# Spreading projection matmuls over the steps of a decoder layer, and loading rows a few steps sooner

## The chip, the cores and the metric

The kernel runs on one core of a Trainium2 chip. The core has five engines that run on their own and meet through semaphores: TensorE (PE in the profile; its weight loads are PEld), VectorE (DVE), ScalarE (ACT), GpSimd (POOL) and SyncE (SP), which here only issues DMAs. The metric is the device time of one execution in microseconds, lower is better.

## The reference: one decoder layer

The layer takes x of 1024 positions by 1024 columns and computes

```
h = rmsnorm(x, mix_pre_norm)
q_a, k_a, v_a, q_h, f_h, i_h, g_h = split(h @ w_in)
attn = rmsnorm(dilated_mixture_attention(q_a, k_a, v_a))       # 8 heads of 64
rec  = hgrn2_recurrence(q_h, f_h, i_h, lower_bound, out_gain) * silu(g_h)   # 4 heads of 128
x = x + rmsnorm(concat[attn, rec] @ w_out)
x = x + rmsnorm(relu(rmsnorm(x) @ w_ff1)^2 @ w_ff2)
```

The attention of a head is a causal softmax over all earlier positions, with a bias per head that holds the three dilated windows and the slope of the head. The recurrence of a head keeps a 128 by 128 state, S_t = diag(f_t) S_(t-1) + (1-f_t) i_t^T, and puts out S_t^T q_t, normalised per head. All is float32.

## The kernel before

**Products.** A product of two float32 matrices is made of three matmuls (`three_pass`, lines 87 to 89): each operand is split into a high part, rounded by a copy on ACT, and a low part, the rest, subtracted on DVE (`split_into`, lines 83 and 84). The weights go through the same: `w_get(i)` makes sure that block i of the stream of weights, and one more, are split, and each split starts the load of the next block (`w_split`, `w_load`). The split weights `wh`, `wl` have two tiles each; some blocks of `w_out` go to tiles that WO_TAG names.

**Order.** The program writes every engine's order out by hand, in the order in which the Python code emits it; no scheduler changes it. Work that has no fixed place, the projections, stands in a `queue` of generators. `fill(ns)` takes pieces off that queue until they add up to ns; each piece is a few matmuls (three of 128x512 are charged 650, three of 128x256 330) and whatever must follow them. What is charged too much or too little is carried over in `debt`. `drain()` takes all that is left at once. A generator that yields None stops the filling until the next call.

**Recurrent heads.** `hgrn_core(h)` works on head h while `fill` spreads the projections of the next head (`hgrn_ig`, `hgrn_qf`) or, in the last head, of the first pair of attention heads (`attn_proj(0)`) between its parts: a fill of 4500, the diagonal products `pd` of the tile `prod` (line 379, 8 products with one column), seven levels of products `pl` (line 393) each with a fill of 2900, the transposes `pk`, the state updates `pu`, the outputs `po` in two banks, and after the norm another fill of 3000. In the last head the first scores of the attention are taken before that fill (`open_attention`).

**Attention.** The 8 heads are worked in 4 pairs, and 64 steps, one for each head and each block b of 128 queries. Step s does, in this order: the exponential of step s+1 on ACT (`raise_`, `expo`), the scores of step s+2 (`look`, `score`: `ps` on PE, then on DVE the bias added and the maximum taken, then its negative `nm`), the transposes of its own exponentials (`turn`: `pt` on PE into two banks of the tag "t", `pth` copied on ACT, `ptl` subtracted on DVE), after every second block the product with the values (`weigh`, `pov`, and its copy `ot`), and the folding and scaling of the one before (`finish`, `anat`). Then come the hooks of that step, and a fill of 2700 - 320 b, or of 1300 in the last pair. A pair ends with block 7 of its second head, so that the steps of a pair are 0 to 15, 16 to 31 and so on, and long blocks stand at the end of each head.

**Projections of a pair.** `attn_proj(pr)` makes queries, values and keys of pair pr, each in two halves of 512 positions and 24 matmuls. After each half DVE scales it (`qf`, `vf`, `kf`), ACT splits off the high parts (`q`, `kh`) and POOL the low ones (`ql`, `kl`), and SP issues small DMAs that lay them out in the other half of the partitions. The next pair's generator is put into the queue two steps before it is needed, when the pair before begins to run out: at s = 14, 30 (and for the first ones by `open_attention`), after a `drain()` that finishes the pair that is about to be scored.

**The recurrent rows.** The outputs of the recurrent heads go to memory (`mix_dram`) and are read back for the output projection. At step 45 `early_open` opens the tiles for the first four blocks of rows in the pool "wide", whose eight tiles hold `hT`, the transposed input, until the last projection is done; it loads the rows, and the bias table of head 7. `row_rec` multiplies them by their gain on POOL, `row_turn` transposes them on PE (`pmt`, also in the banks of tag "t") and splits them into `emt`, and `early_out` multiplies them with the first four blocks of `w_out` (`pwe`). These products are the filling of the last pair's steps.

The rest (the output projection, and the two products of the feed-forward part, from 585 us on) is written by other functions that the change does not touch.

Of the kernel before, what the change touches and what calls it, by code (L numbers as in the profile page):

```python
# [8 lines left out]
F32 = mybir.dt.float32  # L9
# [8 lines left out]
P = 128  # L18
# [7 lines left out]
AH = 8  # L26
# [9 lines left out]
def hymba_layer(ctx, tc, x, w_in, w_out, w_ff1, w_ff2, g_pre, lb_logits, g_mix, g_post,  # L36
# [21 lines left out]
    def half(name, dtype=F32):  # L58
        return sp.tile([P, 512], dtype, tag="half", name=name, bufs=2)
# [91 lines left out]
    for i in range(4 * HH, 4 * HH + 3 * (AH // 2)):  # L151
        stream.append((w_in[i], None))
    WO0 = len(stream)
    WO_TAG = (None, None, ("S", "S"), ("S", "BT"), ("S", "S"), ("S", "T"), ("T", "T"), ("T", "T"))

    def wo_dest(k, tags):
        return lambda: (slab(tags[0], f"woh{k}", F32R), slab(tags[1], f"wol{k}", F32R))
# [215 lines left out]
    def hgrn_core(h, scale, after=None):  # L373
        hd = heads[h]
        inat, gate, prod, qt, kt, tot = (hd[n] for n in ("inat", "gate", "prod", "qt", "kt", "tot"))
        fill(4500 * scale)
        pd = bank("t", f"pd{h}")
        for c in range(NT):
            TE.matmul(pd[:, c:c + 1], prod[:, c * P:(c + 1) * P], ones, start=True, stop=True)
# [3 lines left out]
        V.tensor_tensor(out=at, in0=ident.unsqueeze(1).to_broadcast([P, NT, P]),  # L383
                        in1=dg.unsqueeze(2).to_broadcast([P, NT, P]), op=ALU.mult)
        cur = tot
        for li, c in enumerate(LEVELS):
            nb = 64 // c
            qv = qt.rearrange("p (b two c) -> p b two c", two=2, c=c)
# [47 lines left out]
        for g4 in range(2):  # L436
            po = bank("pv", f"po{h}_{g4}").rearrange("p (n c) -> p n c", n=4)
            for j in range(4):
                n = g4 * 4 + j
                TE.matmul(po[:, j], at[:, n], inat[:, n], start=True, stop=n == 0)  # L440
                if n > 0:
                    TE.matmul(po[:, j], qt[:, n * P:(n + 1) * P], st[:, n], start=False, stop=True)
            g = slice(g4 * 4, g4 * 4 + 4)
            S.activation(sq[:, g], po, AF.Square)
            V.tensor_reduce(ss[:, g], sq[:, g], axis=AX.X, op=ALU.add)  # L445
            pos.append(po)
        rsqrt_mean(rs, ss, P, NT)
        if after is not None:
            after()
        fill(3000 * scale)  # L450
        for n in range(NT):
            V.scalar_tensor_tensor(gate[:, n], pos[n // 4][:, n % 4], rs[:, n:n + 1], gate[:, n],
                                   op0=ALU.mult, op1=ALU.mult)
# [8 lines left out]
    def attn_proj(pr):  # L462
# [48 lines left out]
        for hf in range(2):  # L511
            sl = slice(hf * 512, hf * 512 + 512)
            n = 0
            for cost in proj_t(w, f"ak{pr}", hf, box):
                n += 1
                if n == 3 and hf == 0:
                    v_turn(*late)
                    cost += 450.0
                yield cost
            full = half(f"kf{pr}{hf}")  # L520
            V.tensor_tensor(out=full, in0=box[0], in1=rrow[:, sl], op=ALU.mult)
            for i, (a, b) in enumerate(halves):
                S.activation(stacks[i]["kh"][a:b, sl], full[a:b], AF.Copy)  # L523
                G.tensor_tensor(out=stacks[i]["kl"][a:b, sl], in0=full[a:b], in1=f32(stacks[i]["kh"][a:b, sl]),  # L524
                                op=ALU.subtract)
            for n in ("kh", "kl"):
                nc.sync.dma_start(out=f32(stacks[0][n][64:128, sl]), in_=f32(stacks[0][n][0:64, sl]))
                nc.sync.dma_start(out=f32(stacks[1][n][0:64, sl]), in_=f32(stacks[1][n][64:128, sl]))
            yield 650.0
        pairs[pr] = (stacks, vs)  # L530

    anats = [None] * (AH // 2)
    bts = {}
# [2 lines left out]

    def load_bias(hd):
        if hd < AH and hd not in bts:
            if hd < AH - 1:
                bts[hd] = slab("BT", f"bt{hd}")  # L540
            else:
                bts[hd] = wide.tile([P, 2, T], F32, tag="A", name=f"bt{hd}")[:, 0]
            nc.sync.dma_start(out=bts[hd], in_=bias_tab[hd])

    def score(hd, b):
# [89 lines left out]
    NE = 4  # L635
    early = {}

    def early_open():
        early["rows"] = wide.tile([P, NE, AW], F32, tag="A", name="erows")
        early["mt"] = [wide.tile([P, 2, 2, 4, P], F32R, tag="A", name=f"emt{q}") for q in range(NE // 2)]  # L640
        load_bias(AH - 1)
        early["sum"] = [wide.tile([P, 2, D], F32, tag="A", name=f"esum{q}") for q in range(NE // 2)]
        nc.sync.dma_start(out=early["rows"],
                          in_=mix_dram[:NE * P, :AW].rearrange("(n p) d -> p n d", p=P))

    def early_sum(t):
        return early["sum"][t // 2][:, t % 2]
# [7 lines left out]
        return early["rows"][:, t] if t < NE else rows[t][:, :AW]  # L655

    def row_rec(t):
        G.tensor_tensor(out=rec_row(t), in0=rec_row(t), in1=gains["gmix"][:, :AW], op=ALU.mult)

    def row_fin(t):  # L660
        return anats[-1][:, t].rearrange("p i d -> p (i d)")
# [155 lines left out]
    for h in range(HH):  # L817
# [6 lines left out]
            drain()  # L824

    hooks = {
        45: lambda: [drain(), load_gain("gmix", "R", g_mix), early_open()],
        46: lambda: w_get(WO0, 0),
        47: lambda: [w_get(WO0 + 1, 0), row_rec(0), row_rec(1)],
        48: lambda: [row_turn(0, 0), w_get(WO0 + 2, 0), row_rec(2), row_rec(3)],  # L830
        49: lambda: [row_turn(1, 0), w_get(WO0 + 3, 0), queue.extend(early_out(t) for t in range(NE))],
        50: lambda: row_turn(2, 0),
        51: lambda: row_turn(3, 0),
        55: lambda: [row_load(t) for t in range(3)],
        59: lambda: [row_norm(0), row_gain(0)],
        60: lambda: [row_norm(1), row_gain(1)],
# [6 lines left out]
    for s in range(n_steps):  # L843
# [10 lines left out]
            to_weigh.append((hd, b // 2))  # L854
        to_fold, last_fold = [(i, g, weigh(i, g)) for i, g in ready], to_fold
        if fresh and s + 2 < n_steps:
            drain()
            if (s + 2) // 16 + 1 < AH // 2:
                queue.append(attn_proj((s + 2) // 16 + 1))
            look(s + 2)  # L860
        for i, g, a in last_fold:
            finish(i, g, *a)
        hooks.get(s, lambda: None)()
        fill(2700.0 - 320.0 * b if s < n_steps - 16 else 1300.0)
    for i, g, a in to_fold:
        finish(i, g, *a)
    to_fold = [(i, g, weigh(i, g)) for i, g in to_weigh]
# [793 lines left out]
```

## Time and profile before

| what | value |
|---|---|
| median of the runs shown | 1316.15 us (1313.2, 1319.82, 1316.15) |
| profiled execution | 1313.2 us, of which the profile's span is 1311.4 |
| PE busy over the span | 1264.5 us (96%) |
| DVE, ACT, POOL busy | 858.7, 515.1, 283.6 us |
| recurrent heads after the first projection | about 65 to 321 us |
| 64 steps of attention | about 321 to 585 us |
| HBM read, written | 106.50 MB, 39.85 MB |

Times in the profile are microseconds from the start of the span. A line of the timeline gives start, duration, engine, line of the program, operation, tile written and tiles read, shapes, and in brackets how long the engine sat idle before it and what released it; a number after an x says how many alike are merged. A line of windows gives a stretch, its length, the busy time of each engine in it with the instructions in brackets, then the granted share of the TensorE clock, the share of the DMA engines and the rate in GB/s. A line of waits says who waited for whom: microseconds in all, how often, the longest.

### The profile page before, as it was taken

Reading aid. Unit: us, or ns where it says so; the run is one execution under the profiler, and the core shown is the slowest. Engines: PE = TensorE matmul, PEld = TensorE weight load, DVE = VectorE, ACT = ScalarE, POOL = GpSimd, SP = SyncE. Lnnn points to the kernel's source line nnn. Section 1 sums busy time; section 2 is a strip of 40 time slices with the busy share of each in tenths; the row PEclk is TensorE's granted clock in tenths of the full one; section 3 lists DMA queues with packets and bytes.
Section 4 is the critical chain, followed back from the end, with each engine's and each line's share of the span. In section 5 each row is a group of like instructions: output and inputs, shape, how many; then the busy total and the mean of one; then the engine's idle time right before and its main releaser. Section 6 shows DMA issues by size and latency. Waiting matters only on the chain. (4 is left out here: it accounts for less than half of the span.)

```text
span 1311.4 us, 17500 instructions
## 1 busy us (share of the span) xinstructions
PE 1264.5 (96%) x6730; PEld 1081.8 (82%) x6730; DVE 858.7 (65%) x1431; ACT 515.1 (39%) x908; POOL 283.6 (22%) x276
## 2 busy tenths in 40 slices
PE   9999999999989999898999899999999999999997
PEld 8898989888878888786887688888887888888886
DVE  5556566675656655666757656666666777688956
ACT  6612121213545554564555422222234633344412
POOL 0000000012011111123432178755651000000002
PEclk9999999999999999899999899999999999999999
DMA  5202020213122222416251444534469453444423
GB/s 203 65 17 65 17 64 17 65 49 98 48 81 65 81 65 59 137 41 215 97 177 58 143 168 169 177 129 140 174 222 347 165 196 115 146 131 128 147 80 130
DMA packets 58563, 153.77 MB, mean 117 GB/s; under 512 B 5104, under 2 KB 13040, under 8 KB 58224
## 3 DMA queue, kind: packets, MB, share of 16 engines
q1 hardware_dynamic: 58480, 152.66, 34.9%
q8 instruction: 53, 0.87, 0.3%
q14 instruction: 30, 0.25, 0.1%
HBM read 106.50 MB, written 39.85 MB: 112 GB/s over the span
## 5 line engine op out<-in xcount | busy, mean ns | idle before, releaser
L88 PE MATMUL f<-bl,ah 128*128 128x512 f32 x392 | 152.6, 389 | 0.5 <-DVE bl L84 0.5
L87 PE MATMUL f<-bh,ah 128*128 128x512 f32 x392 | 152.6, 389 | 0.4 <-ACT acc L1441 0.4
L89 PE MATMUL f<-bh,al 128*128 128x512 f32 x392 | 152.5, 389 | 0.0
L84 DVE TENSOR_TENSOR al<-ar,ah 128x1024 fp32r<-128x1024 f32 x49 | 60.7, 1239 | 49.6 <-ACT ah L83 21.7
L88 PEld LDWEIGHTS f<-bl,ah 128*128 128x128 f32 x392 | 73.6, 188 | 16.1 <-DVE bl L84 0.8
L87 PEld LDWEIGHTS f<-bh,ah 128*128 128x128 f32 x392 | 73.6, 188 | 16.0 <-ACT acc L1441 0.9
L89 PEld LDWEIGHTS f<-bh,al 128*128 128x128 f32 x392 | 73.6, 188 | 15.3
L83 ACT ACTIVATE ah<-ar 128x1024 fp32r<-128x1024 f32 x49 | 52.3, 1067 | 54.1 <-PE f L89 25.3
L566 DVE CUSTOM_DVE_ANT_0 p<-ps,bt 128x512 f32<-128x512 f32 (+2 forms) x96 | 50.6, 552 | 31.7 <-PE ps L564 31.5
L1577 POOL TENSOR_SCALAR fp<-fss 128x1 f32<-128x1 f32 x8 | 3.5, 432 | 268.8 <-ACT fd L1574 268.8
L594 DVE TENSOR_TENSOR ptl<-pt,pth 128x512 fp32r<-128x512 f32 (+2 forms) x96 | 50.2, 551 | 16.4 <-ACT pth L593 16.3
L593 ACT ACTIVATE pth<-pt 128x512 fp32r<-128x512 f32 (+2 forms) x96 | 43.3, 486 | 42.0 <-PE pt L590 41.8
L590 PE MATMUL pt<-ident,p 128*128 128x128 f32 x288 | 43.6, 279 | 11.6 <-DVE ptl L594 11.6
L393 PEld LDWEIGHTS pl<-qt,kt 128*128 128x128 f32 x448 | 52.9, 192 | 1.5 <-PE pm_av L89 0.9
L393 PE MATMUL pl<-qt,kt 128*128 128x64 f32 x448 | 53.5, 272 | 0.5 <-DVE qt L399 0.5
L577 ACT ACTIVATE p<-p,nm 128x128 f32<-128x128 f32 (+3 forms) x64 | 49.5, 773 | 10.0 <-DVE nm L572 5.7
L524 POOL TENSOR_TENSOR kl<-kf,kh 64x512 fp32r<-64x512 f32 x16 | 20.4, 1274 | 151.3 <-ACT kh L523 150.7
L231 ACT ACTIVATE inat<-pig,rstd 128x128 f32<-128x128 f32 x32 | 11.6, 367 | 95.4 <-PE pig L89 82.3
L590 PEld LDWEIGHTS pt<-ident,p 128*128 128x128 f32 x288 | 33.7, 142 | 17.2 <-DVE ptl L594 14.2
L83 ACT ACTIVATE bh<-br 128x1024 fp32r<-128x1024 f32 x28 | 29.9, 1067 | 41.1 <-PE f L89 35.8
L79 POOL TENSOR_SCALAR ms<-hss 128x8 f32<-128x8 f32 x4 | 0.8, 196 | 203.6 <-DVE hss L445 203.6
L84 DVE TENSOR_TENSOR wl<-raw,wh 128x1024 fp32r<-128x1024 f32 x23 | 31.3, 1359 | 18.0 <-ACT wh L83 18.0
(1584 smaller groups left out, 3848.9 us busy)
## 6 DMA issues: line engine op xcount, KB each, us to landing
ar<-actd SPq DMA_DIRECT2D x49, 512.0 KB, 3.7
raw<-in_w_in_dram SPq DMA_DIRECT2D x28, 512.0 KB, 3.7
w1r<-in_w_ff_dram SPq DMA_DIRECT2D x14, 1024.0 KB, 6.5
br<-in_w_ff_dram SPq DMA_DIRECT2D x14, 1024.0 KB, 6.5
actd<-e SPq DMA_DIRECT2D x17, 768.0 KB, 4.2
actd<-e SPq DMA_DIRECT2D x11, 1024.0 KB, 4.1
xr<-in_x_dram SPq DMA_DIRECT2D x8, 512.0 KB, 9.0
bt<-in_bias_tab_dram SPq DMA_DIRECT2D x8, 512.0 KB, 4.3
```

The source lines that it names most:

```text
L83: S.activation(hi, src, AF.Copy)
L84: eng.tensor_tensor(out=lo, in0=src, in1=f32(hi), op=ALU.subtract)
L87: TE.matmul(dst, lhs[0], rhs[0], start=start, stop=False)
L88: TE.matmul(dst, lhs[0], rhs[1], start=False, stop=False)
L89: TE.matmul(dst, lhs[1], rhs[0], start=False, stop=stop)
L393: TE.matmul(pl[:, n * 64:(n + 1) * 64], kt[:, n * P:(n + 1) * P], qv[:, n * nb:(n + 1) * nb, 1, :], start=True, stop=True)
L524: G.tensor_tensor(out=stacks[i]["kl"][a:b, sl], in0=full[a:b], in1=f32(stacks[i]["kh"][a:b, sl]), op=ALU.subtract)
L566: V.tensor_tensor_reduce(out=pe[:, k0:k0 + n], in0=pS[:, :n], in1=bts[hd][:, o:o + n], scale=1.0, scalar=-3.0e38, op0=ALU.add, op1=ALU.max ...
L577: S.activation(pe[:, :nk], pe[:, :nk], AF.Exp, bias=nm[:, b:b + 1], accum_out=dn[:, b:b + 1])
L590: TE.transpose(pt[:, j * P:(j + 1) * P], pe[:, jj * P:(jj + 1) * P], ident)
L593: S.activation(hi, src, AF.Copy)
L594: V.tensor_tensor(out=lo, in0=src, in1=f32(hi), op=ALU.subtract)
```

## The change

It has three parts. In `hgrn_core` two fills are cut in two: 2200 before the products `pd` and 2300 after them, in place of 4500 before; 1500 between the two banks of `po` and 1500 after the norm, in place of 3000 after. In the steps, the fill is 3400 - 360 b in place of 2700 - 320 b, up to step 43, and 1000 in the steps 44 to 47; a pair counts as there once the first half of its keys is projected, and the steps wait with a loop of small fills for that, in place of draining. And the tiles and loads for the recurrent rows come when the first half of the last pair's keys is projected, as that frees half of `hT`'s tiles; their gain is loaded with them into half of the tile that later takes the bias table; the scaling, the transposes and the early products come one to two steps sooner, and the weight blocks of `w_out` change tiles.

```diff
-    WO_TAG = (None, None, ("S", "S"), ("S", "BT"), ("S", "S"), ("S", "T"), ("T", "T"), ("T", "T"))
+    WO_TAG = (None, ("S", "S"), None, ("S", "BT"), ("S", "S"), ("S", "T"), ("T", "T"), ("T", "T"))
...
     def hgrn_core(h, scale, after=None):
...
-        fill(4500 * scale)
+        fill(2200 * scale)
         pd = bank("t", f"pd{h}")
...
         cur = tot
+        fill(2300 * scale)
         for li, c in enumerate(LEVELS):
...
             pos.append(po)
+            if g4 == 0:
+                fill(1500 * scale)
         rsqrt_mean(rs, ss, P, NT)
         if after is not None:
             after()
-        fill(3000 * scale)
+        fill(1500 * scale)
...
     def attn_proj(pr):
...
+            if hf == 0 and pr == AH // 2 - 1:
+                early_rows()
             full = half(f"kf{pr}{hf}")
...
+            pairs[pr] = (stacks, vs)
             yield 650.0
-        pairs[pr] = (stacks, vs)
...
     def load_bias(hd):
         if hd < AH and hd not in bts:
-            if hd < AH - 1:
-                bts[hd] = slab("BT", f"bt{hd}")
-            else:
-                bts[hd] = wide.tile([P, 2, T], F32, tag="A", name=f"bt{hd}")[:, 0]
+            bts[hd] = slab("BT", f"bt{hd}") if hd < AH - 1 else early["table"][:, 0]
...
-    def early_open():
+    def early_rows():
         early["rows"] = wide.tile([P, NE, AW], F32, tag="A", name="erows")
+        early["table"] = wide.tile([P, 2, T], F32, tag="A", name="etable")
         early["mt"] = [wide.tile([P, 2, 2, 4, P], F32R, tag="A", name=f"emt{q}") for q in range(NE // 2)]
-        load_bias(AH - 1)
+        gains["early"] = early["table"][:, 1, :AW]
+        nc.sync.dma_start(out=gains["early"], in_=g_mix[:AW].partition_broadcast(P))
+        for q in range(NE // 2):
+            nc.sync.dma_start(out=early["rows"][:, 2 * q:2 * q + 2],
+                              in_=mix_dram[2 * q * P:2 * (q + 1) * P, :AW].rearrange("(n p) d -> p n d", p=P))
+
+    def early_sums():
         early["sum"] = [wide.tile([P, 2, D], F32, tag="A", name=f"esum{q}") for q in range(NE // 2)]
-        nc.sync.dma_start(out=early["rows"],
-                          in_=mix_dram[:NE * P, :AW].rearrange("(n p) d -> p n d", p=P))
...
     def row_rec(t):
-        G.tensor_tensor(out=rec_row(t), in0=rec_row(t), in1=gains["gmix"][:, :AW], op=ALU.mult)
+        gain = gains["early"] if t < NE else gains["gmix"][:, :AW]
+        G.tensor_tensor(out=rec_row(t), in0=rec_row(t), in1=gain, op=ALU.mult)
...
     hooks = {
-        45: lambda: [drain(), load_gain("gmix", "R", g_mix), early_open()],
-        46: lambda: w_get(WO0, 0),
-        47: lambda: [w_get(WO0 + 1, 0), row_rec(0), row_rec(1)],
-        48: lambda: [row_turn(0, 0), w_get(WO0 + 2, 0), row_rec(2), row_rec(3)],
-        49: lambda: [row_turn(1, 0), w_get(WO0 + 3, 0), queue.extend(early_out(t) for t in range(NE))],
-        50: lambda: row_turn(2, 0),
-        51: lambda: row_turn(3, 0),
+        45: lambda: [row_rec(0), row_rec(1)],
+        46: lambda: [w_get(WO0, 0), row_rec(2), row_rec(3)],
+        47: lambda: [row_turn(0, 0), w_get(WO0 + 1, 0), load_bias(AH - 1)],
+        48: lambda: [drain(), load_gain("gmix", "R", g_mix), early_sums(), w_get(WO0 + 2, 0), row_turn(1, 0),
+                     queue.extend(early_out(t) for t in range(NE))],
+        49: lambda: [w_get(WO0 + 3, 0), row_turn(2, 0)],
+        50: lambda: row_turn(3, 0),
...
         if fresh and s + 2 < n_steps:
-            drain()
+            while pairs[(s + 2) // 16] is None:
+                fill(1.0)
             if (s + 2) // 16 + 1 < AH // 2:
+                drain()
                 queue.append(attn_proj((s + 2) // 16 + 1))
             look(s + 2)
...
-        fill(2700.0 - 320.0 * b if s < n_steps - 16 else 1300.0)
+        fill(3400.0 - 360.0 * b if s < n_steps - 20 else 1000.0 if s < n_steps - 16 else 1300.0)
```

## The prediction, made before the changed kernel ran

> **What bounds the kernel now.** I read the page's first two parts, then busy times by stage, then the waits of TensorE (PE) in the attention stage, then the timeline at the longest of them.
>
> ```profile
> PE 1264.5 (96%) x6730; PEld 1081.8 (82%) x6730; DVE 858.7 (65%) x1431; ACT 515.1 (39%) x908; POOL 283.6 (22%) x276
> PEclk9999999999999999899999899999999999999999
> ```
>
> PE is the bound, and the total of its work is not touched: the change only reorders. So the only thing to win or lose is PE's idle time and the stretches in which its clock is granted at half (the two 8s are such slices).
>
> ```profile
> core 0: us, PE busy (x) PEld busy (x) DVE busy (x) ACT busy (x) POOL busy (x), PEclk, DMA share, GB/s
> 195.00:260.00 65.00, 65.00 (x469) 60.95 (x469) 39.94 (x74) 12.70 (x22) 1.83 (x2) 1.00 0.13 38
> 260.00:321.00 61.00, 59.61 (x359) 52.21 (x358) 37.66 (x63) 15.95 (x25) 12.91 (x10) 1.00 0.24 66
> 321.00:388.00 67.00, 59.95 (x358) 51.59 (x357) 42.48 (x135) 35.04 (x77) 10.21 (x8) 1.00 0.25 66
> 388.00:456.00 68.00, 64.14 (x385) 55.86 (x385) 40.55 (x133) 34.91 (x77) 10.26 (x8) 0.99 0.25 71
> 456.00:525.00 69.00, 66.05 (x379) 57.62 (x378) 38.30 (x131) 33.85 (x75) 10.27 (x8) 0.95 0.25 73
> 525.00:585.00 60.00, 54.27 (x336) 48.39 (x335) 39.11 (x123) 37.89 (x91) 11.40 (x18) 0.93 0.25 83
> ```
>
> One recurrent head (195 to 260) has no idle PE at all: nothing can be won in the heads. The four pairs of attention heads (321 to 585, 16 steps each) have some 20 us of idle PE and 0.05 to 0.07 of the clock missing in the last two.
>
> ```profile
> PE pt L590 <- DVE ptl L594: 11.6, 7, 2.8
> PE pmt L698 <- POOL erows L658: 4.7, 1, 4.7
> PE ps L563 <- DVE mx L566: 2.3, 1, 2.3
> ```
>
> PE waits for VectorE (DVE) to empty a bank of transposes (ptl), mostly where one pair ends, and once for the recurrent rows to be loaded and scaled (erows). One such wait, in the pair's step 13, matters for everything below:
>
> ```profile
> 370.28 0.82 PE L590 MATMUL pt<-ident,p 128*128 128x128 f32 x6
> 370.29 1.28 ACT L523 ACTIVATE kh<-kf 64x512 fp32r<-64x512 f32 x2 [1.72 <-DVE kf L521]
> ...
> 371.60 1.04 ACT L577 ACTIVATE p<-p,nm 128x896 f32<-128x896 f32 x1
> ...
> 372.64 0.85 ACT L593 ACTIVATE pth<-pt 128x512 fp32r<-128x512 f32 x2
> 373.25 1.02 DVE L594 TENSOR_TENSOR ptl<-pt,pth 128x512 fp32r<-128x512 f32 x2 [1.53 <-ACT pth L593]
> ...
> 374.00 0.33 PE L590 MATMUL pt<-ident,p 128*128 128x128 f32 x1 [1.75 <-DVE ptl L594]
> ```
>
> Step 12 ended with the last 6 matmuls of a half of the keys. ScalarE then splits that half (kh), takes the next exponential, and only then copies this step's transposes (pth); DVE subtracts (ptl), and the next step's transposes get their bank: 3.72 us from 370.28 to 374.00, however little PE has to do. Last, the clock:
>
> ```profile
> 454.00:456.00 2.00, 0.51 (x3) 0.52 (x4) 1.97 (x7) 0.60 (x2) 0.00 (x0) 0.62 0.72 154
> 456.00:458.00 2.00, 2.00 (x11) 2.00 (x11) 1.37 (x9) 0.28 (x1) 0.00 (x0) 0.50 1.02 381
> ...
> 520.00:522.00 2.00, 0.18 (x2) 0.00 (x0) 0.63 (x2) 2.00 (x5) 1.56 (x2) 1.00 0.69 159
> 522.00:524.00 2.00, 1.88 (x12) 1.84 (x12) 1.44 (x9) 0.98 (x4) 0.00 (x0) 0.68 0.72 179
> ```
>
> Granted over every microsecond, the clock falls to 0.50 during a wait of 3.0 us (452.5) and just after one of 2.1 (520.0), but not after 3.0 (384.6), 2.4 (333.8) or 1.9 (372.1): two of five waits of 1.9 to 3.0 us. What I call the excess of a step is the sum of PE's start-to-start times over the median of their form (227 ns for 128x512, 120 for 128x256, 109 for a transpose); an ordinary step has about 0.16. By it the first dip cost 2.5 us (step 32), the second 1.0.
>
> **The change, part by part.** Steps are numbered 0 to 63 over the eight heads. Matmul counts per step come from the instruction order of the two kernels.
>
> *Heads.* The products pd start 21 matmuls earlier (21 x 0.120 = 2.5 us: 67.8 instead of 70.28 in head 0). They read prod, whose second half ends at 68.57. Four of the eight read the first half and last until 68.6 (the eight took 1.70), so PE waits some 0.1 to 0.2 in three heads, 0.4 in all. Each new break between small and large products costs one late weight load (the first two large ones after pl start 202 ns apart, not 120): 7 x 0.085 = 0.6. Nothing comes back, since PE never waited there. **+1.0** (0.6 to 3).
>
> *Pair 0, steps 0 to 3.* Before PE's 2.45 us wait in step 3 there are now 63 projection matmuls, not 57: 1.36 us more cover. But pt of step 2 and pov now come before their exponentials (the queries' copies stand ahead of them on ACT), so I take half: **-0.7** (0 to -1.4).
>
> *End of pair 0.* Before, step 13 had 3 projection matmuls, step 14 had 21 in a burst and 6 of the next pair, step 15 none: waits of 1.9 and 3.0. The second arose because DVE, idle during the burst, then met kf, the weight split wl (2.0 us) and the scores at once. Now step 12 has 6, step 13 none, steps 14 and 15 six each. kf and kh no longer meet wl; in step 15 the first ptl ends some 2.4 us after the transposes start, and PE has 0.9 of transposes, 0.45 of folds, 1.4 of matmuls and 0.35 of scores as cover, so the 3.0 goes. What is late next is step 13 itself. It is the copied situation above with nothing to fill it: 3.72 minus 0.65 of transposes and 0.37 of folds = 2.7 idle. **-2.2** (2.7 - 4.9).
>
> *End of pair 1.* Before: 30 matmuls in a burst, wait 3.0, dip 2.5. Now the same bare step: **-2.8**.
>
> *End of pair 2 and the rows.* Before, excess over the ordinary in steps 45 to 50: 0, 2.1, 0.9, 6.2 (of it 4.9 for erows), 1.0, 0.4 = 10.6. The loads of rows, gain and table (1.25 MB) now stand on SP's queue in step 42, behind the last matmul that reads the first half of hT; the eight stack copies of the keys queue behind them, and are wanted in step 46, some 12 us later, which covers a landing of 7.5 us (erows). If that cover failed, its 4.9 would return. On POOL the four row_rec (1.27 each) stand behind kl and ahead of nothing before step 59. So the wait for erows goes. What is late next: the bare step 45, 2.7; step 47's transposes of rows, which need a third bank of a kind that has two, and so wait for ptl of step 47, 1.2 by adding ACT's exponential (0.6), pth (1.1) and ptl (0.7) to the end of ptl of step 46; and step 49, where the early products, a step sooner, ask for the fourth weight block in the step that splits it (ACT 1.05, DVE 1.2 behind scores and ptl), 2.6. Sum 6.5: **-4.1** (-7 to -1).
>
> *Other.* Steps 21 and 37 wait 1.2 each for ptl behind the value weights' wl; the split now falls in steps 18 and 34, where wl meets POOL's ql (2.0 instead of 1.2) and holds back the scores some 0.9: **-0.6** in all (-2.4 to +1). With the early products done sooner, the last fold has no matmuls ahead of it and waits for the copy ot (0.38 and two hand-overs): **+0.7**. The swapped weight tiles and the table's load at step 47, wanted in step 54, issue the same DMAs with seven steps as cover: 0; without it at most one landing, 4.3.
>
> *The clock.* The three bare steps idle 2.7 us each, longer than the shortest wait that drew a dip (1.9) and shorter than the longest that did not (3.0). I take two dips at the mean of the prices seen, 1.75: **+3.5** (0 to 7.5). [...]
>
> Sum: 1.0 - 0.7 - 2.2 - 2.8 - 4.1 - 0.6 + 0.7 + 3.5 = -5.2. The profiled execution took 1313.2 (span 1311.4), so 1308.0. It is the fastest of the three shown (median 1316.15); I add nothing for that, since the long waits that escaped a dip in it (384.6, 333.8) are gone or shorter.
>
> **The rivals.** *No dips* (0.20): 2.7 us is ridden out, as three of five waits were, one of them longer. 1308.0 - 3.5 = 1304.5. [...] *The waits only move* (0.20): each bare step dips at the dearer 2.5 (+4.0) and pair 0's start gains nothing (+0.7): 1312.7. For it: the step-13 chain is copied, not shortened. Against: three separate removed waits. *Slower, by the clock at the pair ends* (0.16): after a bare step come transposes and short products only, and PE may not be dense enough to get its clock back. Low for three windows (10.2 us) at half speed costs 5.1 per boundary, 15.4 in place of 3.5: 1319.9. It decides from 7.8 us of low clock per boundary (8.15 + 3.5 = 11.65 over three, doubled). For it: of the four dips inside the kernel (from 454.5, 522.7, 529.6 and 741.2) three lasted 6.8 us and one 3.4. Against: none lasted longer.
>
> **How the numbers follow.** Forecast 0.44, 1308, its own range 1304 to 1312. For all cases 1302 to 1320: below it a part of no dips with every bound at its best, above it the dragging clock's worse half. About half a per cent is what a measurement of this kernel can tell from no change, 6.6 us: faster means under 1309.6, slower over 1322.7. Faster: 0.27 of the forecast and 0.19 of no dips, 0.46. Slower: most of the dragging clock and a little of the unseen, 0.14. Same: 0.40.
>
> **What would show it.** Right: no idle PE before pd beyond 0.2 us; the third-last step of pairs 0, 1 and 2 bare of projection matmuls and 3.7 us long; no wait for erows; a wait of pwe for the fourth weight block near step 49. Wrong: bare steps with another length; a clock at half for more than 7 us; heads over 65.5 us each; the 3.0 us wait for ptl still there at the pair's end.

## The result, and the profile after

The changed kernel takes 1310.1 us (median of 22 runs, 1307.5 to 1314.5); the kernel before took 1315.5 on the same chips (median of 22, 1310.5 to 1324.3). The ratio is 0.9956 with an interval of 0.9943 to 0.9968: 5.4 us between the medians, less than the half per cent that counts as a change here. The profiled execution took 1311.6 us (span 1309.8), only 1.6 less than that of before. The first part of the page, and the clock by 40 slices:

```profile
PE 1265.8 (97%) x6730; PEld 1083.8 (83%) x6730; DVE 859.2 (66%) x1431; ACT 517.0 (39%) x908; POOL 283.2 (22%) x276
PEclk9999899999999999999999999999999999999999
```

The work is the same, and the low slice of the clock has moved: it now stands in the fifth slice, in the recurrent heads, where the kernel before had none. By stage (start and end, length, busy PE, PEld, DVE, ACT, POOL with instructions, granted clock, DMA share, GB/s):

```profile
195.00:261.00 66.00, 64.99 (x469) 60.85 (x468) 39.97 (x76) 12.58 (x22) 1.93 (x3) 1.00 0.11 37
261.00:324.60 63.60, 62.22 (x370) 54.34 (x369) 40.86 (x72) 15.89 (x25) 11.62 (x10) 1.00 0.27 75
324.60:391.00 66.40, 62.99 (x364) 54.70 (x363) 42.50 (x135) 35.83 (x78) 11.02 (x9) 0.97 0.27 74
391.00:460.00 69.00, 65.59 (x385) 57.39 (x384) 40.67 (x131) 35.65 (x78) 10.24 (x8) 0.98 0.25 68
460.00:529.00 69.00, 64.79 (x387) 56.77 (x386) 40.97 (x135) 35.18 (x78) 15.23 (x12) 0.98 0.29 81
529.00:585.00 56.00, 53.28 (x339) 46.67 (x337) 39.05 (x121) 38.97 (x92) 7.30 (x14) 1.00 0.23 77
```

Attention begins 3.6 us later than before (first transposes at 324.65 instead of 321.05), although nine matmuls of 512 columns fewer (2.05 us) stand ahead of it. A recurrent head, which had no idle PE, has 1.01 in the first line. Each of the first three pairs has 0.02 to 0.03 of its clock missing. PE's waits (who waited, for whom, microseconds, times, longest):

```profile
PE pt L592 <- DVE ptl L596: 7.5, 3, 2.5
PE ps L565 <- DVE mx L568: 2.7, 3, 0.9
PE pd L379 <- DVE prod L369: 1.9, 2, 1.0
PE pmt L708 <- issue: 1.3, 2, 0.8
PE pwe L88 <- DVE wol L84: 0.8, 1, 0.8
```

The waits for ptl fell from 11.6 in seven to 7.5 in three, the wait for erows is gone, and two waits for prod are new, as are two before pmt. A wait for prod stands in the middle of the eight products pd, of which the last four read its second half; here it is in head 1 (a product is two records):

```profile
132.94 0.95 PE L379 MATMUL pd<-ones,prod 128*128 128x1 f32 x8
134.82 1.49 PE L379 MATMUL pd<-ones,prod 128*128 128x1 f32 x8 [0.94 <-DVE prod L369]
```

The three waits for ptl are the bare steps 13, 29 and 45, those without projection matmuls. Step 29 in the timeline:

```profile
448.74 0.81 PE L592 MATMUL pt<-ident,p 128*128 128x128 f32 x6
448.75 1.28 ACT L528 ACTIVATE kh<-kf 64x512 fp32r<-64x512 f32 x2 [1.72 <-DVE kf L526]
...
450.06 1.04 ACT L579 ACTIVATE p<-p,nm 128x896 f32<-128x896 f32 x1
...
451.10 0.85 ACT L595 ACTIVATE pth<-pt 128x512 fp32r<-128x512 f32 x2
451.71 1.02 DVE L596 TENSOR_TENSOR ptl<-pt,pth 128x512 fp32r<-128x512 f32 x2 [1.52 <-ACT pth L595]
...
452.46 1.56 PE L592 MATMUL pt<-ident,p 128*128 128x128 f32 x7 [2.51 <-DVE ptl L596]
```

From the first transposes to the next it is 3.72 us, with the chain of before in the same order: kh, the exponential, pth, ptl. From the start of PE's last fold to the next transposes 2.67 us are lost, in each of the three steps. The granted clock is 0.5 from 384.4, 452.7 and 521.0 for 3.41 us each, right behind the first two of these waits and 0.6 us before the end of the third, and for 6.83 us from 135.3, behind the first new wait for prod. I call such a stretch at half clock a dip.

### The profile page after: what moved, and what is told of

Read it like the earlier page. It is cut to its first block, busy times and chain, and to the rows that moved or that the text cites. A ratio compares the mean times of both kernels' runs of the same rounds, so it can differ in the third digit from the quotient of the medians.

```text
span 1309.8 us, 17500 instructions
## 1 busy us (share of the span) xinstructions
PE 1265.8 (97%) x6730; PEld 1083.8 (83%) x6730; DVE 859.2 (66%) x1431; ACT 517.0 (39%) x908; POOL 283.2 (22%) x276
## 5 line engine op out<-in xcount | busy, mean ns | idle before, releaser
L568 DVE CUSTOM_DVE_ANT_0 p<-ps,bt 128x512 f32<-128x512 f32 (+2 forms) x84 | 44.3, 552 | 25.4 <-PE ps L566 25.2
L398 DVE TENSOR_TENSOR kt<-kt,tot 128x512 f32<-128x512 f32 x28 | 20.2, 721 | 37.3 <-PE pl L394 37.3
L84 DVE TENSOR_TENSOR wl<-raw,wh 128x1024 fp32r<-128x1024 f32 x23 | 31.4, 1364 | 19.7 <-ACT wh L83 19.7
```

What stands on the lines that cost most here:

```text
L84: eng.tensor_tensor(out=lo, in0=src, in1=f32(hi), op=ALU.subtract)
L568: V.tensor_tensor_reduce(out=pe[:, k0:k0 + n], in0=pS[:, :n], in1=bts[hd][:, o:o + n], scale=1.0, scalar=-3.0e38, op0=ALU.add, op1=ALU.max ...
```

## Experiments

All ratios are to the kernel before, run on the same chip. Each run also states its mean granted clock; the time at half clock, in the last column, is twice what is missing of it times the span, a mean over the runs of the kernel. In four sets of the kernel before (11 to 22 runs each) it was 29 to 33 us. Over the 22 runs of the changed kernel the time of a run goes with it: the correlation is 0.85, and a us at half clock stands for 0.43 us of time.

| kernel | median us | ratio (95%) | us at half clock |
|---|---|---|---|
| changed kernel | 1310.1 | 0.9956 (0.9943 to 0.9968) | 23.7 |
| only steps and rows changed | 1304.1 | 0.9913 (0.9889 to 0.9937) | 20.0 |
| only the heads changed | 1316.9 | 1.0003 (0.9986 to 1.0019) | 32.0 |
| po split undone | 1304.3 | 0.9901 (0.9881 to 0.9921) | 18.2 |
| bare steps covered, 512 columns | 1305.9 | 0.9923 (0.9902 to 0.9944) | 17.0 |
| bare steps covered, one column | 1310.2 | 0.9950 (0.9927 to 0.9973) | 27.4 |
| keys' last six matmuls in the bare steps | 1305.2 | 0.9921 (0.9900 to 0.9943) | 23.0 |
| rows loaded late | 1310.6 | 0.9963 (0.9949 to 0.9976) | 26.4 |
| early products at step 49 | 1309.6 | 0.9957 (0.9942 to 0.9973) | 26.4 |
| the parts combined | 1296.2 | 0.9835 (0.9812 to 0.9857) | 15.5 |

**The heads' fills whole again.**

```diff
-        fill(2200 * scale)
+        fill(4500 * scale)
...
-        fill(2300 * scale)
...
-            if g4 == 0:
-                fill(1500 * scale)
...
-        fill(1500 * scale)
+        fill(3000 * scale)
```

> The changed kernel with the heads' fills whole again (4500 ahead of pd, 3000 after the norm), so that only the steps and the rows are changed. Theory A (both splits of the heads together cost more than my +1.0): the waits of 1.1 us before pd in heads 1 and 2, and the dip of the clock near 135 us, go; 2.2 of waits, 0.6 of breaks and up to 3.1 of the dip make it 2.8 to 5.9 us faster than the changed kernel, 1304 to 1307 where that one takes 1310; the first transposes of attention start near 321 instead of 324.7 us. Rival B (the heads' splits cost only their breaks, and the later start of attention has another cause): 0.6 faster, and attention still starts near 324.

Measured: 0.9913, 0.43 of a per cent or 5.7 us under the changed kernel. No wait before pd, no dip near 135, attention starts at 322.4. Theory A holds: the heads' splits are worth a loss of the size of the whole gain. The start of attention would be earlier still but for a dip that stands in head 3 of this profile, at 269.3 for 3.41 us, where PE was never idle:

```profile
266.00:268.00 2.00, 2.00 (x19) 2.00 (x20) 0.98 (x3) 1.25 (x2) 0.77 (x1) 1.00 0.75 221
268.00:270.00 2.00, 2.00 (x15) 1.81 (x15) 2.00 (x2) 0.00 (x0) 1.93 (x2) 0.83 0.28 80
270.00:272.00 2.00, 2.00 (x6) 1.53 (x5) 2.00 (x3) 0.00 (x0) 0.71 (x1) 0.50 0.23 51
```

Ahead of it stand the eight products pd with one column and the eight pl with 64, 3.5 us of them without a break (265.60 to 269.09). I come back to that.

**The heads' splits alone, on the kernel before.**

```diff
-        fill(4500 * scale)
+        fill(2200 * scale)
...
+        fill(2300 * scale)
...
+            if g4 == 0:
+                fill(1500 * scale)
...
-        fill(3000 * scale)
+        fill(1500 * scale)
```

> The kernel before with both splits of the heads' fills and nothing else. Theory A: 2.8 to 5.9 us slower than before, waits of about 1.1 us before pd in some heads, and a dip of the clock by them. Rival B: 0.6 to 1.0 slower, no wait before pd over 0.2.

Measured: 1.0003, within -1.8 and +2.5 us of no change. The waits of theory A are there (1.09 and 1.15 before pd in heads 1 and 2, dips of 3.41 us from 135.6 and 203.9), its loss is not. The attention of this kernel gives the waits back: with nine more projection matmuls left for it, the wait in step 3 is 1.75 instead of 2.45 and the 1.92 at the end of pair 0 is gone, 2.6 in all against 2.2 lost. At the end of pair 2 the wait for the rows is 0.7 longer and one of 0.9 is new, so that by the waits 1.2 us of loss are left, which the error of the ratio can't tell from nothing. In the changed kernel the steps already have that filling, and nothing is given back. So the parts do not add up: the same edit costs nothing that could be measured on one kernel and some 6 us on the other.

**Each split alone.** The one after the norm is left whole in the first, the one at pd in the second, both on the kernel before.

```diff
-        fill(4500 * scale)
+        fill(2200 * scale)
...
+        fill(2300 * scale)
```

> The kernel before with the split of the fill at pd alone (2200 ahead, 2300 behind); the fill after the norm is whole again. Theory A (it is the other split, between the two banks of po, that makes prod late): prod ends where it did in the kernel before, and PE waits no more than 0.2 us before pd in any head. Rival B (the pd split alone is enough): waits of about 1.1 us before pd in heads 1 and 2, as in the changed kernel.

```diff
+            if g4 == 0:
+                fill(1500 * scale)
...
-        fill(3000 * scale)
+        fill(1500 * scale)
```

> The kernel before with the split of the fill at po alone (1500 between the banks, 1500 after the norm). Theory A: prod of heads 1 and 2 ends about 1.1 us later than in the kernel before, counted from the start of the head's filling, and pd, which stands at its old place, does not wait for it. Rival B: prod is not later, and the 1.1 us come from pd's place alone.

One run each, for the trace (1316.0 and 1313.4 us). The two writes of prod in head 1, with the start of the first and the last at the end, in the kernel with the split at pd alone:

```profile
L369 DVE TENSOR_TENSOR prod<-qt,kt x2: 691/692/693, 129.1 to 132.8; 128x512 f32<-128x512 f32 x2
```

and in the one with the split at po alone:

```profile
L369 DVE TENSOR_TENSOR prod<-qt,kt x2: 692/692/693, 130.5 to 134.2; 128x512 f32<-128x512 f32 x2
```

Theory A holds on both. With the pd split alone prod stands where it stood before (129.2 to 132.9) and PE does not wait; with the po split alone prod is 1.3 us later and pd, at its old place, comes later still. The wait needs both. DVE and POOL show why prod is late. In the kernel before:

```profile
119.48 0.69 DVE L445 TENSOR_REDUCE hss<-ysq 128x4 f32<-128x512 f32 x1 [1.04 <-ACT ysq L444]
120.53 1.64 POOL L80 TENSOR_TENSOR hrs<-ms,nhalf 128x8 f32<-128x8 f32 x1
122.41 2.36 DVE L84 TENSOR_TENSOR wig2l<-raw,wig2h 128x1024 fp32r<-128x1024 f32 x2 [0.26 <-ACT wig2h L83]
124.69 2.16 DVE L452 SCALAR_TENSOR_TENSOR gate<-po,hrs,gate 128x128 f32<-128x128 f32 x8
```

and in the changed kernel:

```profile
120.83 2.36 DVE L84 TENSOR_TENSOR wig2l<-raw,wig2h 128x1024 fp32r<-128x1024 f32 x2 [0.25 <-ACT wig2h L83]
123.11 0.68 DVE L446 TENSOR_REDUCE hss<-ysq 128x4 f32<-128x512 f32 x1
123.87 0.20 POOL L79 TENSOR_SCALAR ms<-hss 128x8 f32<-128x8 f32 x1 [77.44 <-DVE hss L446]
124.15 1.64 POOL L80 TENSOR_TENSOR hrs<-ms,nhalf 128x8 f32<-128x8 f32 x1
125.82 1.38 DVE L455 SCALAR_TENSOR_TENSOR gate<-po,hrs,gate 128x128 f32<-128x128 f32 x5 [2.04 <-POOL hrs L80]
```

The filling between the two banks of po brings the next head's weight split (wig2l, 2.36 us) ahead of the second sum of squares, which before came at 119.48. The norm's 1.64 us on POOL, which had other work of DVE beside it, is now waited for (2.04 idle), the gates start at 125.82 instead of 124.69, and everything behind them on DVE, prod at its end, is 1.1 us late.

**The po split undone in the changed kernel.**

```diff
-            if g4 == 0:
-                fill(1500 * scale)
...
-        fill(1500 * scale)
+        fill(3000 * scale)
```

> The changed kernel with the fill after the norm whole again (3000), so that of the heads only the split at pd is kept. Theory A (of the heads only the split at po did harm, by making prod 1.1 to 1.3 us later): no wait before pd over 0.2 us in any head, and 4 to 7 us faster than the changed kernel, 1303 to 1306, like the kernel with both fills whole. Rival B (the split at pd costs by itself, by its breaks and by the clock): 1307 to 1310. On the clock: in ten traces the clock was at half after a window of 3.41 us in which the columns of PE's matmuls filled less than about 0.38 of it; with 2300 of filling between pd and the first pl no window of the heads should fall under that, so no dip between 60 and 320 us.

Measured: 0.9901, as fast as with both fills whole within the error; no wait before pd, and no dip between 60 and 320 us. The least share of columns in a window of the heads was 0.42. Theory A holds: the pd split is harmless, the po split is what cost. The gain on the changed kernel is 5.8 us by the medians and 7.2 by the ratios, as the kernel before took longer on this chip (1318.1). Of it 2.2 are the waits in the heads, and 1.2 come from pair 0, whose waits are then 1.32 and 1.22 instead of 1.07 and 2.66; 5.5 us less at half clock (18.2 for 23.7), at the granted 0.5, are worth up to 2.8 by my estimate: 6.2 in sum, as near as two chips allow.

**What draws the clock down.** First nine matmuls of 512 columns in each bare step:

```diff
+        if s % 16 == 13 and s < n_steps - 16:
+            idle = bank("mm", f"idle{s}")
+            for _ in range(9):
+                TE.matmul(idle, part(hT, 0, 1)[0][:, :P], part(hT, 0, 1)[0],
+                          start=True, stop=True)
```

> The changed kernel with nine matmuls of 128x512 more (2.0 us, their output is used by nothing) in each of the bare steps 13, 29 and 45. They take none of the other engines' work away, so the step stays 3.7 us long, but PE idles 0.6 in place of 2.7. Theory A (the idling of 2.7 draws the dip of 3.41 us that follows each bare step): the three dips go, 1.3 to 1.6 us each, and it is about 4.4 us faster than the changed kernel although it does more. Rival B (the dips come from the thin steps after, or from a rhythm of their own): the dips stay, and it takes as long as the changed kernel or is up to 1 us slower.

Measured: 0.9923, so 4.3 us less than the changed kernel with 6 us of matmuls more in it, and none of the three dips. The steps are as long as before. Step 29 of the changed kernel, from 449, in stretches of 2 us (the clock is the third number from the end):

```profile
449.00:451.00 2.00, 0.95 (x10) 0.81 (x7) 1.15 (x5) 1.95 (x3) 1.46 (x2) 1.00 0.22 49
451.00:453.00 2.00, 0.54 (x4) 0.55 (x5) 1.29 (x5) 2.00 (x6) 1.06 (x1) 0.93 0.63 148
453.00:455.00 2.00, 2.00 (x11) 2.00 (x10) 1.13 (x3) 1.17 (x3) 0.00 (x0) 0.50 0.82 176
```

and the same stretch with the nine matmuls:

```profile
449.00:451.00 2.00, 1.63 (x12) 1.20 (x12) 1.47 (x5) 1.93 (x5) 0.48 (x1) 1.00 0.55 127
451.00:453.00 2.00, 2.00 (x17) 1.87 (x16) 1.68 (x6) 1.22 (x4) 0.00 (x0) 1.00 0.96 239
453.00:455.00 2.00, 2.00 (x17) 1.87 (x15) 1.35 (x2) 1.44 (x4) 0.00 (x0) 1.00 0.15 57
```

What theory A asked for came, and rival B falls. That it is the idling is not shown by this, since the nine matmuls also stream columns. And the kernel with the heads' fills whole has two bare steps with the same wait of 2.67 us, and no dip behind either. Its step 29:

```profile
442.00:444.00 2.00, 0.69 (x7) 0.55 (x5) 0.90 (x5) 1.95 (x5) 1.72 (x2) 1.00 0.32 74
444.00:446.00 2.00, 0.80 (x8) 0.80 (x8) 1.47 (x5) 1.93 (x5) 0.80 (x1) 1.00 0.57 130
446.00:448.00 2.00, 2.00 (x18) 1.96 (x17) 1.42 (x4) 1.22 (x4) 0.00 (x0) 1.00 0.93 220
```

The dips of one trace start at whole multiples of 3.413 us from one another: in the changed kernel 73, 93, 113, 142 and 178 of them after the one at 135.27, and from the last, at 742.84, the figure follows, (742.84 - 135.27) / 178 = 3.413. The phase of this grid is another in each trace (the dip at 454.47 in the kernel before lies 93.5 of them after 135.27). So I cut the first six traces along their grids and asked each window what PE had streamed in it: 0.443 ns for each column of a matmul (227 ns for 512), and double for tiles of up to 128 columns (113 ns for 128, where a transpose takes 109), over 3.413 us. The doubling was chosen on these six; the seven traces taken later are cut by the same measure. All thirteen, from 12 us on:

| share of columns in a window at full clock | windows | next window at half |
|---|---|---|
| under 0.375 | 72 | 72 |
| 0.375 to 0.405 | 7 | 4 |
| over 0.405 | 4753 | 0 |

A window at half stays there by the same bound (24 of 24 under 0.375, none of 63 over 0.405). In these windows it is not idling that counts, and the pd products, busy for 1.7 us with eight columns, are as good as a gap. The decisive run covers the bare steps with such products:

```diff
+        if s % 16 == 13 and s < n_steps - 16:
+            idle = bank("mm", f"idle{s}")
+            for c in range(9):
+                TE.matmul(idle[:, c:c + 1], f32(part(hT, 0, 1)[0][:, :P]), ones, start=True, stop=True)
```

> The changed kernel with nine products of one column more (1.9 us at the 212 ns that one takes in pd; their output is used by nothing) in each of the bare steps 13, 29 and 45: PE idles 0.7 in place of 2.7, as with the nine matmuls of 512 columns, but next to nothing is streamed through it. Theory A (what draws the clock down is a window of 3.41 us with few columns in it, whether PE is busy or not): the dips stay, mostly one per bare step, and it takes as long as the changed kernel, ratio 0.995 to 0.997 to the kernel before. Rival B (it is PE's idling): the dips go, and the ratio is that of the kernel with the nine large matmuls, 0.992.

Measured: 0.9950, as slow as the changed kernel, with a dip behind each bare step (383.8, 452.1, 520.3). PE is busy and the clock goes all the same:

```profile
449.00:451.00 2.00, 1.95 (x18) 1.87 (x17) 0.46 (x2) 1.97 (x6) 1.93 (x2) 1.00 0.33 77
451.00:453.00 2.00, 1.50 (x10) 1.50 (x11) 1.39 (x6) 1.87 (x4) 0.10 (x1) 0.77 0.89 202
453.00:455.00 2.00, 2.00 (x11) 2.00 (x11) 1.05 (x3) 0.34 (x1) 0.00 (x0) 0.50 0.76 246
```

Rival B falls. The windows with the bare steps have shares of columns of 0.39, 0.18 and 0.26 here, and of 0.67 and more with the nine large matmuls. In these traces the columns per window decide, not the busy time. The doubling for small tiles is a fit, and why they count so is open.

**The keys' last six matmuls in the bare steps.**

```diff
-        fill(3400.0 - 360.0 * b if s < n_steps - 20 else 1000.0 if s < n_steps - 16 else 1300.0)
+        fill(0.0 if s % 16 == 12 and s < n_steps - 16 else
+             3400.0 - 360.0 * b if s < n_steps - 20 else 1000.0 if s < n_steps - 16 else 1300.0)
```

> The changed kernel with no filling in steps 12, 28 and 44, so that the last six matmuls of a half of the keys fall in steps 13, 29 and 45 and no step is bare. Theory A (the bare step is a chain of PE's fold, the keys' split, the exponential, pth and ptl with nothing beside it): with no split of the keys ahead of the exponential in step 13 and 1.4 us of matmuls in it, its wait falls from 2.7 to under 0.6 and its dip goes; 6 to 10 us faster than the changed kernel. Rival B (the wait goes one step on, since the keys' split then stands ahead of step 14's exponential): waits of 1.5 to 2.7 in steps 14, 30 and 46, within 2 us of the changed kernel.

Measured: 0.9921, 4.6 us under the changed kernel by the ratios, below what A asked for and above what B did. Steps 13, 29 and 45 have no wait left. One step on it is 0.71 in steps 14 and 30, which have six matmuls of the next pair's queries, and 2.10 in step 46, which has none. There rival B is right; the keys' split again stands ahead of the exponential:

```profile
513.19 1.28 ACT L528 ACTIVATE kh<-kf 64x512 fp32r<-64x512 f32 x2 [1.91 <-DVE kf L526]
...
514.50 1.15 ACT L579 ACTIVATE p<-p,nm 128x1024 f32<-128x1024 f32 x1
...
517.00 0.80 PE L592 MATMUL pt<-ident,p 128*128 128x128 f32 x5 [1.94 <-DVE ptl L596]
```

The chain in step 46 is that of the bare steps. The wait went with the filling that PE has in the step after the last matmul of a half of the keys: 2.67 and 2.10 us with none, 0.71 with six matmuls.

**The rows.** First the changed kernel with its third part undone; the loads, the tiles and the weight blocks go back with these lines.

```diff
-            if hf == 0 and pr == AH // 2 - 1:
-                early_rows()
...
-        45: lambda: [row_rec(0), row_rec(1)],
-        46: lambda: [w_get(WO0, 0), row_rec(2), row_rec(3)],
-        47: lambda: [row_turn(0, 0), w_get(WO0 + 1, 0), load_bias(AH - 1)],
...
+        45: lambda: [drain(), load_gain("gmix", "R", g_mix), early_open()],
+        46: lambda: w_get(WO0, 0),
+        47: lambda: [w_get(WO0 + 1, 0), row_rec(0), row_rec(1)],
+        48: lambda: [row_turn(0, 0), w_get(WO0 + 2, 0), row_rec(2), row_rec(3)],
...
```

> The changed kernel with its third part undone: rows and table loaded at step 45, scaled, transposed and multiplied at the old steps, the weight blocks in the old tiles. Theory A (my term for the end of pair 2 and the rows): the wait for erows is back with 4 to 5 us in step 47 or 48, the waits of 1.0 (pmt) and 1.8 (pwe) near 527 and 535 go, and it is 1.5 to 5 us slower than the changed kernel, 1312 to 1315. Rival B (the drain at step 45 has nothing left to drain now, so the load goes out as early as PE needs it): no wait for erows over 1, and the time is within 1 us of the changed kernel.

Measured: 0.9963, the same as the changed kernel within the error. The wait for the rows is back with half its size:

```profile
PE pmt L701 <- POOL erows L661: 2.4, 1, 2.4
```

Neither expectation is met in full: A's wait came at half its size and its loss did not come; B's time came, but not its wait of at most 1. With the projections spread, the third part has 2.6 us of waits to remove (2.58 from start to start) and brings 0.97, 0.64, 0.76, 1.03 and 0.70 of its own. It is worth nothing that these runs could tell from zero.

Then the changed kernel with the early products a step later:

```diff
-        48: lambda: [drain(), load_gain("gmix", "R", g_mix), early_sums(), w_get(WO0 + 2, 0), row_turn(1, 0),
-                     queue.extend(early_out(t) for t in range(NE))],
-        49: lambda: [w_get(WO0 + 3, 0), row_turn(2, 0)],
+        48: lambda: [drain(), load_gain("gmix", "R", g_mix), early_sums(), w_get(WO0 + 2, 0), row_turn(1, 0)],
+        49: lambda: [w_get(WO0 + 3, 0), row_turn(2, 0), queue.extend(early_out(t) for t in range(NE))],
```

> The changed kernel with the early products put into the queue at step 49 instead of 48, all else the same. Theory A (the products ask for the fourth weight block before it is split): the waits of 0.76 and 1.03 between pwe in step 49 go, and the 0.7 of the last fold, which gets matmuls ahead of it again; 1.5 to 2.5 us faster than the changed kernel, 1307.6 to 1308.6. Rival B: step 48 is then bare and waits for its transposes by as much, no change.

Measured: 0.9957, no difference. The waits of pwe and of the last fold go, as A says, but a wait of 0.69 for transposes (from 531.4) comes, and the one of 0.64 for the rows' transposes is 1.28 (from 532.8), with a dip at 534.8: rival B.

**The parts combined.** The po split undone and no filling in steps 12, 28 and 44, which had helped when run alone; early products at step 49, which alone had changed nothing; later transposes of the rows and other fills in seven steps, which had not been run alone:

```diff
-        47: lambda: [row_turn(0, 0), w_get(WO0 + 1, 0), load_bias(AH - 1)],
-        48: lambda: [drain(), load_gain("gmix", "R", g_mix), early_sums(), w_get(WO0 + 2, 0), row_turn(1, 0),
-                     queue.extend(early_out(t) for t in range(NE))],
-        49: lambda: [w_get(WO0 + 3, 0), row_turn(2, 0)],
-        50: lambda: row_turn(3, 0),
+        47: lambda: [w_get(WO0 + 1, 0), load_bias(AH - 1)],
+        48: lambda: [drain(), load_gain("gmix", "R", g_mix), early_sums(), w_get(WO0 + 2, 0), row_turn(0, 0)],
+        49: lambda: [row_turn(1, 0), w_get(WO0 + 3, 0), queue.extend(early_out(t) for t in range(NE))],
+        50: lambda: row_turn(2, 0),
+        51: lambda: row_turn(3, 0),
...
-        fill(3400.0 - 360.0 * b if s < n_steps - 20 else 1000.0 if s < n_steps - 16 else 1300.0)
+        spread = {9: 2390.0, 10: 2030.0, 40: 2700.0, 42: 2030.0, 44: 0.0, 45: 1300.0, 46: 1300.0}
+        fill(spread[s] if s in spread else 0.0 if s % 16 == 12 and s < n_steps - 16 else
+             3400.0 - 360.0 * b if s < n_steps - 20 else 1000.0 if s < n_steps - 16 else 1300.0)
```

> What the runs so far point to, together: the fill after the norm whole, the split at pd kept, no filling in steps 12, 28 and 44 with six key matmuls in each of 13, 29 and 45 and six more in 46, rows loaded early, but transposed and multiplied at the old steps. Theory A (each of the waits that were seen is a thing of its own): the 2.7 of the bare steps go to at most 0.8, step 46's too, the waits of 0.97, 0.64, 0.76, 1.03 and 0.7 at the rows go, and the three dips with them: 8 to 12 us under the kernel with both fills whole (1304.1), 1292 to 1296. Rival B (the waits move on, to steps 47 to 49 or to the weight splits): 1299 to 1304.

Measured: 0.9835 (0.9812 to 0.9857), 1296.2 us on a chip where the kernel before took 1318.1: 1.65% faster than before and 1.2% faster than the changed kernel. Its waits:

```profile
PE pt L590 <- DVE ptl L594: 3.0, 3, 1.9
PE ps L563 <- DVE mx L566: 1.8, 2, 0.9
PE pmt L706 <- DVE emt L84: 1.8, 1, 1.8
```

Theory A holds for pairs 0 and 1 (0.71 and 0.72 left in steps 14 and 30). At the end of pair 2 rival B has its part: the wait is now in step 47 (2.08), and one of 1.94 for the rows' transposes is new in step 49. The dips of the bare steps are gone for pairs 0 and 1; this profile has two others, 3.41 us each from 512.7 and 519.5, beside these two waits.

## Why the prediction was right, and where it was wrong

The median lies 2.1 us above the predicted 1308.0, inside the 1304 to 1312 of the forecast itself; the gain falls short of the half per cent (1309.6) by half a microsecond, so that "the same" came, with 0.40, and not "faster", with 0.46. Of the signs named, the bare steps of 3.7 us, the gone wait for erows and the wait of pwe came as said; idle PE before pd and heads over 65.5 us (from pd to pd 65.1, 69.2 and 66.5, where the kernel before has 65.0 to 65.4) spoke against it. Point by point:

- *Heads, +1.0: the step that failed.* PE waits 1.08 and 1.15 us before pd in heads 1 and 2, and not 0.4 in all. I took prod's end from the trace of before and gave the po split no cost; it moves prod by 1.1 to 1.3. Beside the 2.2 of waits, the 6.83 us at half clock from 135.3 cost 3.1 in this execution, counted as the prediction counts excess. My 0.6 for seven breaks can't be seen: counted at full clock and with equal work, attention starts 2.2 later (324.65 - 321.05 - 3.4 + 2.05), which the two waits fill. Undoing the po split alone is worth 5.8 us by the medians, 7.2 by the ratios.
- *Pair 0, steps 0 to 3, -0.7.* Better: the wait of 2.45 is 1.07, so all of the 1.36 of cover counted and not half.
- *End of pair 0, -2.2; end of pair 1, the wait.* Right: bare steps of 3.7 us with 2.67 idle in place of 1.92 + 3.00, and of 3.01.
- *End of pair 2 and the rows, -4.1: too much.* The new waits were sized well (2.67, 0.97 for 1.2, and 0.64 + 0.76 + 1.03 = 2.4 for 2.6). The old side was not: the 10.6 of excess that I set against them held 3.65 for the dips from 522.7 and 529.6 as well, and dips came back at other places. By waits alone it is 6.95 (2.09 + 4.86) against 6.07, -0.9. And most of it belongs to the spreading; the early load by itself is worth nothing that was measured.
- *Other.* Steps 19 and 35 wait 1.07 each (0.9 predicted) in place of 1.18; the last fold 0.70 (0.7).
- *The clock, +3.5 for two dips.* All three bare steps dipped, at 1.3 to 1.6 instead of 1.75 each, 4.4 in all, and the dip near 135 was not in the sum. The rival without dips was no less possible: the same 2.67 us drew none in the kernel with the heads' fills whole, where a window's border cut the wait (shares of columns 0.70 and 0.46), and over the 22 runs of the changed kernel the time at half clock went from 18 to 32 us. Nor did every dip follow idle time: the one at 269.3 in the kernel with the heads' fills whole stands where PE was never idle.

By waits over 0.6 us, without two of about 1.0 that both kernels have, the attention went from 19.7 to 15.3 and the heads from 0 to 2.2, so -2.2 in all. The forecast has much the same once clock and waits are kept apart. Its terms set 2.5 (pair 1) and 3.65 (end of pair 2) of old dips down as gone; without these, and without the +3.5 for new ones, -2.55 is left for waits. In it the heads are 1.2 too cheap, and pair 0's start and the end of pair 2 gain 1.1 more than I said. For the clock the same sum has 3.5 - 2.5 - 3.65 = -2.65. The two profiled executions show nothing of that gain: 27.7 us at half in the changed kernel and 27.5 before, as the dip near 135 and three at bare steps stand in place of the old ones, and they differ by -1.6.

The medians differ by more, -5.4, and the clock fits that: over the runs the changed kernel spends 23.7 us at half and the kernel before 29 to 33 in its four sets, worth 2.8 to 4.7 us at the granted 0.5, by my estimate. (For the set beside which the changed kernel was measured no clock was kept.) So the -5.2 came in size, in part by luck: the heads cost more, pair 0 and the rows less, and the dip near 135, which I had not foreseen, is outweighed by a clock that over the runs is better than in the one profiled execution. Why it is better there is not shown; that the long waits of before (3.0, 3.0, 4.9) are shorter or gone may be the reason. The 2.1 us by which the median lies above the forecast come from where I started, the profiled execution, 2.3 below the median of before. I had added nothing for that; its clock was better than the mean (27.5 us at half, for 29 to 33 in the sets).

The rival that ended slower, a clock dragged down for three windows per pair, did not come: each bare step drew one window, 3.41 us. Its chance was also booked wrongly, since its own 1319.9 lies below the 1322.7 from which the prediction calls a time slower, so most of the 0.14 for slower belonged to "the same". That the waits only move came in part, at the rows (6.07 for 6.95) and in two of the experiments.

## What to carry to other kernels

Before filling is moved, follow what else the filling emits: here the cost of a split lay in a weight subtraction (2.36 us) that it put ahead of a short reduction on VectorE (0.68 us), and showed some 12 us later as a wait on PE (1.08 us before pd in head 1). In these traces a bare spot was told by the matmul columns streamed in a window of 3.41 us and not by idle time: half clock followed all 72 windows with a share under 0.375 and none of 4753 over 0.405, while 2.67 us of idle PE drew a dip in three steps of the changed kernel and none in two of the kernel with the heads' fills whole. Small products stood ahead of two of the dips: the eight pd with a wait of 1.08 us among them (dip at 135.3), and eight pd and eight pl in a row, 3.5 us with no wait (dip at 269.3). A single profile is one draw of the clock, as the 18 to 32 us at half clock over the 22 runs of one kernel show; the mean granted clock over many runs tells what a change did to it.

## What was not expected of the hardware

- In the thirteen traces the clock was at half in the next window of 3.413 us after all 72 windows at full clock whose share of columns, by the measure above, was under 0.375, after 4 of the 7 from 0.375 to 0.405, and after none of the 4753 above. PE's busy time did not tell them apart: from 449 to 453 us it was 1.49 of 4.00 in the changed kernel and 3.45 with the nine one-column products, and the dip followed in both (452.7, 452.1).
- So a wait of 1.08 us, far below a window's length, came with a dip where small products stood beside it (among the pd products: share 0.30 in the window from 131.9, half clock from 135.3), and a wait of 2.67 us went free where a border of windows cut it (shares of columns 0.70 and 0.46 in the two windows from 440.0 and 443.4 of the kernel with the heads' fills whole, no dip).
- Nine one-column products in a bare step changed the time by nothing measurable (0.9950 for 0.9956), and nine of 512 columns there saved 4.3 us (0.9923), while the step was 3.7 us long with both, as without them.
